# Loading the first and fourth conditioning blocks in two pieces each, with fewer constant products at the head

## The chip, the cores and the metric

The kernel runs on one NeuronCore of a Trainium2 chip. A core has five engines that run at the same time: TensorE (PE in the profile, with its weight loads as PEld), VectorE (DVE), ScalarE (ACT), GpSimd (POOL) and SyncE (SP). Sixteen DMA engines move data between HBM and the core's memory SBUF. A queue of loads is issued by SP, a few by ACT and POOL. The metric is device time in microseconds (us) of one execution; lower is better.

## The reference

One inference step of a one-layer decoder, for 256 prompt tokens and 8 x 4 sample tokens (T = 288 columns in the kernel), model width 2048, everything in float32:

```python
def _layer(x, c, conv_prefix, chunk, ...):
    mod = (jax.nn.silu(c) @ w_ada + b_ada).reshape(n, N_MOD, 1, D_MODEL)
    sh_m, sc_m, gt_m, sh_f, sc_f, gt_f = [mod[:, i] for i in range(N_MOD)]
    h = _rms(x, g_mix) * (1 + sc_m) + sh_m
    proj = h @ w_in                      # 2048 x 9216
    b_gate, c_gate, hc, u, v, ga, gb = jnp.split(proj, idx, axis=-1)
    z = c_gate * hc
    conv = sum(w_conv[k] * zfull[:, k:k + s] for k in range(CONV_WIDTH))
    ya = b_gate * conv
    ...                                  # yb: gated spatial mixing of u and v
    merged = jax.nn.sigmoid(ga) * (ya @ w_pa) + jax.nn.sigmoid(gb) * (yb @ w_pb)
    x = x + gt_m * (merged @ w_out)
    h2 = _rms(x, g_ffn) * (1 + sc_f) + sh_f
    gate, up = jnp.split(h2 @ w_ffn_in, 2, axis=-1)
    x = x + gt_f * ((jax.nn.silu(gate) * up) @ w_ffn_out)
    return x, conv_state, v_rows
```

There are nine conditioning vectors `c` (one for the prompt, eight for the samples). `silu(c) @ w_ada` is 9 x 2048 by 2048 x 12288; the rest of the layer needs its columns as scales, shifts and gates.

## The kernel before

Activations lie with features on the 128 partitions and tokens along the free dimension. Every large product is made in three passes: weight and activation are each cut into a high part (a copy rounded to fp32r) and a low part (the rest), and PE adds high x high, high x low and low x high in PSUM. ACT casts the high part (`hi`), DVE subtracts for the low part (`lo`).

The weights stream from HBM in blocks. Blocks of `w_in` are called wA, wB, wC, wE, wD (`Blk`), those of `w_ada` aA, aB, aC, aE, a2 to a5 (`Ada`). A block is loaded into one of five buffers named `raw` (RAW = 5). The list `steps` gives the order of the blocks and of the work between them (`Do`). A load is issued five blocks ahead of its use. Up to the step `free`, the instructions of DVE and ACT keep the order in which the code issues them, and those of SP do so still longer (`Pinned`); PE's order is chained as well (`S["pe"]`, `strict`). Behind these points the framework orders what is not chained.

The head is what the change touches:

- `ct`, the nine vectors (128 x 144), is loaded by ACT's queue. `silu` makes `cs` of it: a tanh on ACT (`ctt`), two instructions on DVE.
- The aA blocks hold the columns of `w_ada` that give the scale and the shift of the first 128 features. There are four, each 128 partitions x 1024 columns (512 KB), and each is used in eight float32 products of 32 x 128 (`Ada.run`, L423), sixteen records in the trace. They go to four groups of 32 columns of PE, and all add into one PSUM tile `ada`.
- `aA[3].out` copies `ada` to `ev` on ACT; `early_weights` makes `b1` from the constants `cp1` and, in `wA[0].first`, `hi` and `lo` of the first 256 columns of the first weight block on DVE; `aA[3].fin` multiplies `ev` by a selection matrix (L456) and makes `gm1` (`gm` in the trace) and `mod` on DVE; `early0` scales the first 128 features of `x` by `gm1` and cuts them into `hi` and `lo` (`s`). Then `wA[0]` (`FirstBlk.run`, L674) makes the first projection products.
- `warm(n)` makes n products of a 128 x 128 matrix of ones with itself (L310), whose result nobody reads. Each stands as two records in the trace. With a second argument it is placed behind that instruction.

SP issues the loads in this order: the four aA blocks, `cp1`, the first 512 columns of wA[0], the first part of `x`, the rest of wA[0], and then the blocks of `steps`.

The functions that the diff touches and what calls them:

Of the kernel before, what the change touches and what calls it, by code (L numbers as in the profile page):

```python
# [68 lines left out]
def decoder_kernel(tc, d):  # L69
    nc = tc.nc  # L70
    with ExitStack() as es:
        def pool(name, bufs=1, **kw):
            return es.enter_context(tc.tile_pool(name=name, bufs=bufs, **kw))

        pc = pool("const")
        pw = pool("wstream")
        pslot = pool("slots", SLOTS)
        ptmp = pool("tmp", 5)
        pps = pool("psum", 4, space=bass.MemoryType.PSUM)
        early = ExitStack()  # L80
        pshort = early.enter_context(tc.tile_pool(name="short", bufs=SHORT, side="right"))

        def reopen():
            early.close()
            return pool("thirds", 2, side="right", reuse_waits="tile")

        _body(tc, nc, d, pc, pw, pslot, pshort, reopen, ptmp, pps)


def _body(tc, nc, d, pc, pw, pslot, pshort, reopen, ptmp, pps):  # L90
    ids = [0]

    def nm(s):
        ids[0] += 1
        return f"{s}_{ids[0]}"
# [4 lines left out]
    def slot(dt=F32, shape=(P, T), short=False):  # L100
        return (pshort if short else pslot).tile(list(shape), dt, tag="s", name=nm("s"), padded_shape=[P, TU])
# [7 lines left out]
    def psmisc():  # L109
        return pps.tile([P, 512], F32, tag="misc", name=nm("px"), bufs=3)  # L110

    def behind(i):
        return tc.issue_after(i.ins) if i is not None else ExitStack()
# [17 lines left out]
    V, A, G, PE, SY = Pinned(nc.vector), Pinned(nc.scalar), nc.gpsimd, nc.tensor, Pinned(nc.sync)  # L131
# [174 lines left out]
    def warm(n, after=None):  # L306
        ps = psmisc()
        with behind(after):
            for _ in range(n):
                PE.matmul(ps[:, :P], ones, ones, start=True, stop=True)  # L310
# [75 lines left out]
    class Ada(Step):  # L386
# [7 lines left out]
        def load(self):  # L394
            self.ks = 2 if self.fb[0] == self.fb[1] else 1
            if self.apart:
                self.raw = [slot(shape=(P, 256)) for _ in range(8)]
                for i, t in enumerate(self.raw):
                    SY.dma_start(t, d[self.name][self.blk][:, 256 * i : 256 * i + 256])
                return  # L400
            n = self.nk * 512 * self.nq // self.ks
            self.raw = pw.tile([P, n], F32, tag="raw", name=nm("raw"), bufs=RAW, padded_shape=[P, 2048])
            SY.dma_start(self.raw, d[self.name][self.blk])

        def split(self):
            pass
# [307 lines left out]
    def ada(name):  # L714
        u = units[name]
        return [(Thirds if name == "a5" else Ada)(u, b) for b in range(16 // u[3])]
# [540 lines left out]
    aA, aB, aC, aE = (ada(n) for n in ("aA", "aB", "aC", "aE"))  # L1257
# [59 lines left out]
        for k in range(1, 4):  # L1317
            mo[k].norm()

    steps = [Do(silu), Do(lambda: warm(10)), *aA[:2], Do(lambda: warm(1, aA[1].last)), aA[2]]  # L1320
    steps += [Do(lambda: warm(2, aA[2].last)), aA[3], Do(lambda: warm(1, aA[3].last)), Do(aA[3].out), Do(early_weights), Do(aA[3].fin), Do(early0)]
    steps += [Do(lambda: warm(5, aA[3].last))] + wA[:4] + aB[:2] + [wA[4], Do(sums1), Do(sums1_out)] + aB[2:4] + [Do(rstd1), wA[5]]
    steps += aB[4:6] + [wA[6], Do(norms)] + aB[6:] + wA[7:] + [Do(free), *wB[:2]]
    steps += aC[:2] + [wB[2], Do(later), rescale(LONG, RAWX, "rbl"), rescale(0, 10, "rbl")] + aC[2:4] + wB[3:4] + [norms_ahead(4, 8)] + begin(wB[4]) + aC[4:6] + wB[4:5] + begin(wB[5]) + aC[6:] + [wB[5], gain(4, 8)]
# [89 lines left out]
    n = len(steps)  # L1414
# [174 lines left out]
```

## Time and profile before

| | |
|---|---|
| median of 3 runs | 1514.07 us (1513.61 to 1514.92) |
| profiled execution, its time | 1513.66 us |
| profiled execution, its span (first to last instruction) | 1511.9 us |
| granted TensorE clock | 0.999 |
| PE busy | 1504.7 us |
| DVE busy | 1060.9 us |
| ACT busy | 776.5 us |
| POOL busy | 176.6 us |
| HBM read | 352.56 MB |

The profile is of one execution. The span runs from the first to the last instruction; the time of an execution is 1.76 us more. Busy time of PE counts every matrix product, useful or not, and products are pipelined, so a busy PE says only that something was in it. In rows of the chain stand start, length, engine, tile, line of the code and the number of records; rows of the timeline add the shapes, and in brackets the idle time before the instruction and what ended it. Line 124 is a helper that most DVE, ACT and SP instructions pass through, so these are told apart by their tiles.

### The profile page before, as it was taken

How to read it: one execution, taken by the hardware profiler on the slowest of the kernel's cores; microseconds unless marked ns; L12 is line 12 of the kernel's file. 1: busy time of each engine (PE TensorE's matmuls, PEld its weight loads, DVE VectorE, ACT ScalarE, POOL GpSimd, SP SyncE). 2: the span in 40 equal slices, each digit the busy share in tenths (PEclk: the TensorE clock that was granted, in tenths of full speed). 3: DMA queues.
4: the chain of work that ended last, by engine and by line, in shares of the span. 5: the costliest groups of instructions: out<-in, count | busy, mean ns of one | idle time of the engine just before them, and what ended most of it. 6: DMA issues, size and time to landing. Idle time of an engine off the chain costs nothing.

```text
span 1511.9 us, 32334 instructions
## 1 busy us (share of the span) xinstructions
PE 1504.7 (100%) x12734; PEld 1449.6 (96%) x12734; DVE 1060.9 (70%) x2099; ACT 776.5 (51%) x1487; POOL 176.6 (12%) x353
## 2 busy tenths in 40 slices
PE   9999999999999999999999999999999999999998
PEld 8898999998899898989999999999999999999998
DVE  6786677978666576667878666666666567675586
ACT  5443354743345444457655455455545454454465
POOL 2555410000030000002500101100010100100000
PEclk9999999999999999999999999999999999999999
DMA  9977876578888778875654657564575745754452
GB/s 390 357 282 301 344 272 219 197 285 313 328 321 311 261 258 299 272 278 204 225 190 163 218 189 244 205 215 142 180 248 183 251 136 178 243 186 157 146 176 98
DMA packets 75689, 357.75 MB, mean 237 GB/s; under 512 B 9248, under 2 KB 28512, under 8 KB 46352
## 3 DMA queue, kind: packets, MB, share of 16 engines
q1 hardware_dynamic: 70384, 337.02, 62.4%
q0 software_dynamic: 5008, 18.59, 3.5%
q8 instruction: 99, 1.62, 0.4%
q14 instruction: 54, 0.44, 0.1%
q10 hardware_dynamic: 144, 0.07, 0.0%
HBM read 352.56 MB, written 3.09 MB: 235 GB/s over the span
## 4 chain that ended last, share of the span: by engine, by line
PE 100%; DVEq 0%; DVE 0%; issue 0%
PE pm L575 30%; PE pm L577 30%; PE pm L576 30%; PE ada L423 5%; PE ada L630 1%; PE px L304 1%; PE px L310 0%; PE pm L690 0%; PE pm L692 0%; PE pm L691 0%; PE pm L674 0%; PE px L733 0%; PE px L692 0%; PE px L691 0%; PE px L690 0%; PE pm L304 0%
## 5 line engine op out<-in xcount | busy, mean ns | idle before, releaser
L575 PE MATMUL pm<-s,hi 128*128 128x288 f32 (+1 forms) x3688 | 1058.1, 287 | 0.0
L577 PE MATMUL pm<-s,lo 128*128 128x288 f32 (+1 forms) x3688 | 1055.0, 286 | 0.0
L576 PE MATMUL pm<-s,hi 128*128 128x288 f32 (+1 forms) x3688 | 1054.9, 286 | 0.0
L124 ACT CAST hi<-raw 128x512 fp32r<-128x512 f32 (+2 forms) x956 | 578.4, 606 | 633.7 <-PE pm L576 547.1
L124 DVE TENSOR_TENSOR lo<-raw,hi 128x512 fp32r<-128x512 f32 (+2 forms) x959 | 657.2, 691 | 333.5 <-ACT hi L124 310.8
L575 PEld LDWEIGHTS pm<-s,hi 128*128 128x128 f32 x3688 | 697.0, 189 | 10.8 <-issue 8.9
L576 PEld LDWEIGHTS pm<-s,hi 128*128 128x128 f32 x3688 | 697.1, 189 | 0.0
L577 PEld LDWEIGHTS pm<-s,lo 128*128 128x128 f32 x3688 | 697.0, 189 | 0.0
L124 DVE TENSOR_TENSOR s<-pm,s 128x288 f32<-128x288 f32 x175 | 78.8, 454 | 24.8 <-PE pm L577 20.5
L594 POOL DMA_DIRECT2D s<-in_a x64 | 34.1, 538 | 344.7 <-PE pm L577 327.2
L423 PE MATMUL ada<-raw,cs 128*32 128x512 f32 (+3 forms) x640 | 61.8, 515 | 0.0
L124 ACT CAST s<-t 128x288 fp32r<-128x288 f32 (+2 forms) x109 | 50.3, 465 | 18.2 <-DVE t L124 15.4
L124 DVE TENSOR_TENSOR s<-t,s 128x288 fp32r<-128x288 f32 (+1 forms) x109 | 50.1, 462 | 10.7 <-ACT s L124 10.4
L124 DVE SCALAR_TENSOR_TENSOR t<-t,pm 128x288 f32<-128x288 f32 x84 | 37.9, 451 | 12.5 <-PE pm L577 8.5
L423 PEld LDWEIGHTS ada<-raw,cs 128*32 128x32 f32 x640 | 18.7, 112 | 25.3 <-issue 17.3
L124 DVE TENSOR_TENSOR s<-s,s 128x256 f32<-128x256 f32 (+2 forms) x96 | 38.4, 430 | 0.5 <-ACT s L124 0.5
L315 POOL TENSOR_TENSOR t<-x,gm 128x32 f32<-128x32 f32 x16 | 7.7, 483 | 262.5 <-DVE acc L124 248.4
L124 ACT CAST s<-s 128x256 bf16<-128x256 f32 (+1 forms) x80 | 29.7, 414 | 1.8 <-DVE s L124 1.8
L803 POOL TENSOR_TENSOR s<-s,rb 128x288 f32<-128x288 f32 x30 | 29.1, 991 | 0.0
L599 POOL DMA_DIRECT2D word<-in_a x8 | 4.4, 549 | 196.4 <-PE ada L630 142.8
L124 DVE SCALAR_TENSOR_TENSOR s<-pm,s 128x288 f32<-128x288 f32 x48 | 24.3, 511 | 2.5 <-PE pm L577 2.5
L124 ACT COPY s<-pm 128x288 f32<-128x288 f32 (+1 forms) x53 | 21.1, 401 | 9.1 <-PE pm L577 8.5
(189 smaller groups left out, 721.2 us busy)
## 6 DMA issues: line engine op xcount, KB each, us to landing
raw<-in_fi SPq DMA_DIRECT2D x84, 1024.0 KB, 4.9
raw<-in_f SPq DMA_DIRECT2D x64, 704.0 KB, 4.1
raw<-in_wD SPq DMA_DIRECT2D x36, 1024.0 KB, 8.3
raw<-in_a SPq DMA_DIRECT2D x32, 1024.0 KB, 5.1
raw<-in_wC SPq DMA_DIRECT2D x20, 896.0 KB, 6.1
raw<-in_aE SPq DMA_DIRECT2D x16, 1024.0 KB, 7.5
s<-in_a SPq DMA_DIRECT2D x128, 128.0 KB, 5.2
raw<-in_wo SPq DMA_DIRECT2D x16, 1024.0 KB, 6.7
```

The lines of the kernel that those rows point to most:

```text
L124: i = f(*args, **kw)
L304: return in_order(op(*args, **kw))
L315: G.tensor_tensor(sam(a[:, TP:T]), sam(x[:, k, TP:]), bc4(gm[:, k, 1:]), ALU.mult)
L423: PE.matmul(acc[32 * j : 32 * j + 32, c], cs9[:, 32 * kt : 32 * kt + 32] if second else cs[:, kt, :], self.raw[2 * j + h] if self.apart el ...
L575: PE.matmul(ps[:, : self.n], wh, ah, start=first, stop=False)
L576: PE.matmul(ps[:, : self.n], wh, al, start=False, stop=False)
L577: self.last = in_order(PE.matmul(ps[:, : self.n], wl, ah, start=False, stop=last))
L594: G.dma_start(w, src[:, 256 * i : 256 * i + 256])
L599: G.dma_start(raw, src)
L630: PE.matmul(acc[32 * j : 32 * j + 32, n * h : n * h + n], S["csr"][:, self.blk, :], w[:, o : o + n], start=self.blk == 0 and p == 0, stop= ...
L803: G.tensor_tensor(a[:, :T], a[:, :T], S[rb], ALU.mult)
```

## The change

The load of an `Ada` block that is not cut into slots is issued in pieces where a table says so: aA[0] as columns 0 to 256 and 256 to 1024, aA[3] as columns 0 to 512 and 512 to 1024. All other blocks are loaded in one piece as before. The number of constant products at the very start goes from ten to eight, and before aA[3] from two to one.

```diff
@@ Ada.load
             n = self.nk * 512 * self.nq // self.ks
             self.raw = pw.tile([P, n], F32, tag="raw", name=nm("raw"), bufs=RAW, padded_shape=[P, 2048])
-            SY.dma_start(self.raw, d[self.name][self.blk])
+            cuts = {("aA", 0): [0, 256, n], ("aA", 3): [0, 512, n]}.get((self.name, self.blk), [0, n])
+            for a, b in zip(cuts, cuts[1:]):
+                SY.dma_start(self.raw[:, a:b], d[self.name][self.blk][:, a:b])
@@ steps
-    steps = [Do(silu), Do(lambda: warm(10)), *aA[:2], Do(lambda: warm(1, aA[1].last)), aA[2]]
-    steps += [Do(lambda: warm(2, aA[2].last)), aA[3], Do(lambda: warm(1, aA[3].last)), Do(aA[3].out), ...
+    steps = [Do(silu), Do(lambda: warm(8)), *aA[:2], Do(lambda: warm(1, aA[1].last)), aA[2]]
+    steps += [Do(lambda: warm(1, aA[2].last)), aA[3], Do(lambda: warm(1, aA[3].last)), Do(aA[3].out), ...
```

More of the change, by code (lines that the diff above doesn't have):

```diff
@@ L1318, in norms @@
             mo[k].norm()
-    steps = [Do(silu), Do(lambda: warm(10)), *aA[:2], Do(lambda: warm(1, aA[1].last)), aA[2]]
-    steps += [Do(lambda: warm(2, aA[2].last)), aA[3], Do(lambda: warm(1, aA[3].last)), Do(aA[3].out), Do(early_weights), Do(aA[3].fin), Do(early0)]
+    steps = [Do(silu), Do(lambda: warm(8)), *aA[:2], Do(lambda: warm(1, aA[1].last)), aA[2]]
+    steps += [Do(lambda: warm(1, aA[2].last)), aA[3], Do(lambda: warm(1, aA[3].last)), Do(aA[3].out), Do(early_weights), Do(aA[3].fin), Do(early0)]
     steps += [Do(lambda: warm(5, aA[3].last))] + wA[:4] + aB[:2] + [wA[4], Do(sums1), Do(sums1_out)] + aB[2:4] + [Do(rstd1), wA[5]]
```

## The prediction

> **What bounds the kernel now.** I read the page's busy table and its chain first, then the chain, the timeline and the DMA issues of the first 12 us, where the change lies.
>
> ```profile
> PE 1504.7 (100%) x12734; PEld 1449.6 (96%) x12734; DVE 1060.9 (70%) x2099; ACT 776.5 (51%) x1487; POOL 176.6 (12%) x353
> PE 100%; DVEq 0%; DVE 0%; issue 0%
> ```
>
> TensorE (PE) is busy for 1504.7 of 1511.9 us and the chain that ends last is PE throughout. So the change can move the end only by as much as it moves the start of the dense work, and only if nothing later takes that back. The head, as the chain tells it (start, length, what):
>
> ```profile
> 1.05 4.63 PE px L310 x20
> 5.69 1.61 PE ada L423 x32
> 7.30 0.42 PE px L310 x2
> 7.72 0.57 PE ada L423 x16
> 8.29 0.64 PE px L310 x4
> 8.93 0.57 PE ada L423 x16
> 9.51 0.42 PE px L310 x2
> 9.93 0.36 PE px L456 x2
> 10.29 1.21 PE px L310 x10
> 11.50 3.18 PE pm L674 x24
> ```
>
> L310 is the constant product (two records each), L423 the conditioning blocks aA (the first row holds aA[0] and aA[1]), L456 the product that puts their result into columns, L674 the first projection block, where the dense work begins. A busy PE here is partly filler, so the chain hides what really sets 11.5. Behind the filler the other engines show it (start, length, engine, instruction, idle before and its releaser):
>
> ```profile
> 4.67 0.32 ACT L124 ACTIVATE ctt<-ct 128x144 f32<-128x144 f32 x1 [2.22 <-DMA ct<-in_c]
> 5.37 0.23 DVE L124 TENSOR_SCALAR cs<-ctt 128x144 f32<-128x144 f32 x1
> 9.22 0.29 DVE L124 CAST hi<-raw 128x256 fp32r<-128x256 f32 x1 [0.53 <-DMA raw<-in_wA]
> 9.55 0.43 DVE L124 TENSOR_TENSOR lo<-raw,hi 128x256 fp32r<-128x256 f32 x1
> 9.57 0.27 ACT L124 COPY ev<-ada 128x128 f32<-128x128 f32 x1 [4.58 <-PE ada L423]
> 10.33 0.23 DVE L124 SCALAR_TENSOR_TENSOR gm<-px,b,cp 128x9 f32<-128x9 f32 x1 [0.35 <-PE px L456]
> 10.59 0.53 ACT L124 ACTIVATE s<-x,gm 128x256 fp32r<-128x256 f32 x1 [0.45 <-DVE gm L124]
> 11.08 0.23 ACT L124 CAST s<-t 128x42 fp32r<-128x42 f32 x1
> 11.36 0.39 PE L674 MATMUL pm<-s,hi 128*128 128x298 f32 x1
> ```
>
> Two chains meet in `gm` at 10.33. One goes from the landing of `ct` over the tanh and `cs` (ready at 5.60) to the four aA blocks, `ev` and L456. The other is VectorE's (DVE's) own order: the first weight block lands, `hi` and `lo` are made (9.22 to 9.98), then `gm`. The first chain is late by 0.35 us today. From `gm` to the first L674 product pass 1.03 us of fixed work.
>
> The loads (issue on SP; then each load with the time from issue to landing):
>
> ```profile
> 0.74 1.80 SPq L124 DMA_DIRECT2D raw<-in_aA  x4
> 2.58 0.54 SPq L124 DMA_DIRECT2D cp<-in_cpack  x1
> 3.17 0.49 SPq L124 DMA_DIRECT2D raw<-in_wA  x1
> 3.70 0.44 SPq L124 DMA_DIRECT2D x<-in_x  x1
> ct<-in_c ACTq DMA_DIRECT2D x1, 72.0 KB, 3.9
> raw<-in_aA SPq DMA_DIRECT2D x1, 512.0 KB, 3.7
> raw<-in_aA SPq DMA_DIRECT2D x1, 512.0 KB, 6.2
> raw<-in_wA SPq DMA_DIRECT2D x1, 256.0 KB, 6.0
> x<-in_x SPq DMA_DIRECT2D x1, 144.0 KB, 5.9
> SPq L124 <- DMA ct<-in_c: 0.5, 1, 0.5
> ```
>
> The 3.7 is aA[0]'s, landed at 4.44; the 6.2 is aA[3]'s, issued last of the four at 2.11 and landed at 8.3; `wA` landed at 3.17 + 6.0 = 9.2, `x` at 9.6. The tanh starts at 4.67, so `ct` landed at about 4.65, only 0.2 after aA[0] though it has a seventh of its bytes. The next view has busy time by engine, then the granted clock, the DMA share and GB/s:
>
> ```profile
> 1.50:2.50 1.00, 1.00 (x7) 1.00 (x7) 0.06 (x1) 0.95 (x1) 0.00 (x0) 1.00 0.69 136
> 2.50:3.50 1.00, 1.00 (x6) 1.00 (x6) 0.00 (x0) 0.00 (x0) 0.00 (x0) 1.00 0.88 315
> 3.50:4.20 0.70, 0.70 (x5) 0.70 (x4) 0.00 (x0) 0.00 (x0) 0.00 (x0) 1.00 1.08 421
> 4.20:9.20 5.00, 5.00 (x73) 4.02 (x76) 0.70 (x3) 0.32 (x1) 0.00 (x0) 1.00 1.02 403
> ```
>
> The DMA engines are full from 3.5 us on: whatever stands in line lands when the bytes ahead of it have passed.
>
> **The change part by part.** *aA[0] in 256 and 768 columns.* `ct` (72 KB) travels beside a first piece of 128 KB instead of 512 KB. The latest it can land is as now, 4.65. The earliest: the windows moved 0.14 MB by 2.5 us, 0.45 by 3.5 and 0.75 by 4.2, so aA[0] and `ct` together (0.60 MB) were through at about 3.85, and `ct` was landed 0.8 later; 0.2 MB would be through at 2.7, landed at 3.5. Its landing beside aA[0]'s says that the two advanced together, row by row, so it should follow the shorter rows, but part of it will meet the 768-column rows. I take the middle, 4.05. From `ct` to aA's first product pass 5.69 - 4.65 = 1.04 us, so that starts at 5.1 (bounds 4.55 and 5.7). The second piece lands with the same bytes as now, about 4.5, in time.
>
> [...]
>
> *Ten constant products become eight.* The first row of the chain gives 4.63 / 20 = 0.23 us a record, so the filler ends 4 x 0.23 = 0.9 earlier, at 4.76. Today it ends at 5.68, `cs` is ready at 5.60: they are level. Eight products leave PE idle from 4.76 to 5.1, and to 5.7 if `ct` does not move. This alone frees nothing.
>
> *Two constant products before aA[3] become one.* 0.64 - 0.42 = 0.22 us out of the aA chain, if aA[3]'s data is there.
>
> *aA[3] in halves.* It lands at 8.3 now, and its products start at 8.93. With the chain 0.6 earlier they would wait; with halves the first 256 KB (0.65 us earlier at 403 GB/s) lets half of them run, and only the second half waits for 8.4.
>
> *Two more loads on SP.* 1.80 / 4 = 0.45 us each, so `cp1`, `wA` and `x` are issued 0.9 later (wA at 4.07). The line of bytes ahead of them covers this: `wA` waits 6 us in line. Uncovered it would cost that 0.9. SP also stood 0.5 us for `ct` before the ninth load (the last row of the loads); with two more that wait meets `wA`'s first piece, at 4.05 against an issue at 4.07: nothing, and 0.6 in the worst case, still 3 us ahead of its turn. What is not covered is the loss from shorter rows. Below, it is nothing or a gain (the bytes are the same, and the start might fill sooner). Above: if the start is paid by rows, the first 128 rows carry 128 KB where they carried 512, and 0.39 MB at 403 GB/s is 0.96 us on every landing behind. I take 0.1, since from 2.5 us on the rate rose to 315 and 421 with `ct`'s short rows in the mix.
>
> *The sum.* aA[0] and aA[1] run at half pace, 0.85 each (a little over half of the 1.61 that their 32 records took, since the pace stepped up at their end): 5.1 to 6.8. Then one product 0.42, aA[2] 0.57, one product 0.42: 8.2. aA[3] ends at the later of 8.2 + 0.57 and its second half's landing 8.4 + 0.4 (half of its work and its tail): 8.8, against 9.5 now. L456 ended at 10.29, 0.8 behind aA[3], so it ends 0.7 earlier, at 9.6. But `gm` stands behind `hi` and `lo`: `wA` at 9.2 + 0.1, then 0.76 of DVE work: 10.08. So `gm` moves by 10.33 - 10.08 = 0.25 us and not by 0.7, and the first L674 product starts at 11.11. The five products behind L456 are then finished well ahead.
>
> Behind that every order stays as it is, and PE is the chain. Loads that could take it back lie between 12 and 52 us, where the DMA engines are full. The tightest I found is the second aB block (issue, its landing after 12.1 us, and the products):
>
> ```profile
> 11.78 0.33 SPq L124 DMA_DIRECT2D raw<-in_aB  x1
> raw<-in_aB SPq DMA_DIRECT2D x1, 768.0 KB, 12.1
> 23.76 1.50 PE L423 MATMUL ada<-raw,cs 128*32 128x384 f32 x16
> ```
>
> It lands at 23.9; its half of the 16 records starts near 24.4. With PE 0.25 earlier and the load 0.1 later, 0.15 or more is left. So the gain is 0.25 us: the profiled execution, 1513.66 (1.76 more than its span), becomes 1513.4; it lies 0.4 below the median of the runs, 1514.07. My time is 1513.8.
>
> **The rivals.** *The deeper gain.* If `wA` lands sooner (a quicker start), `gm` follows L456: 0.7 less, 1513.4. For it: the first chain really is 0.7 shorter. Against: `wA` stands behind 2.1 MB in a full line. Chance 0.1.
>
> *Nothing arrives.* `ct` lands as now, aA starts at 5.7, and of the first chain only the 0.22 is left; L456 ends at 10.07 and `gm` runs at 10.1. Oddly that is the forecast's time too, since DVE decides; if short rows cost 0.35 us instead of 0.1, it is 1514.1, no change. Chance 0.22.
>
> *Slower by the start of the loads.* The upper bound above, 0.96 us on `wA`: `hi` at 10.2, `gm` at 10.95, 0.6 later than now: 1514.7. It decides from a delay of 0.35 us on. For it speaks the slow first microsecond (136 GB/s), against it that `ct`'s 576-byte rows passed in that same stretch. Chance 0.15.
>
> *Slower by PE's pace.* The granted clock in the rows reads 1.00 throughout, yet ten records of the constant product took 1.21 us after 10.3 and 2.3 (20 in 4.63) before 5.7: PE runs at half pace until some point during aA[1]. The idle stretch that eight products leave may put that point off. At half pace from 5.1 to the end of aA: 6.8 for two blocks, about 0.65 for each product with its switch, 0.85 for aA[2] and aA[3]: 9.8, `gm` at 10.6, 0.3 later than now; if it reaches into L674's 24 products (3.18 us), up to 3.2 more. So 1514.4 to 1517.6. Chance 0.13. [...]
>
> **How the numbers follow.** Forecast 0.40, the others as given: 1.0. The lowest run shown, 1513.61, less 0.9 for the deeper gain gives 1512.7; the highest, 1514.92, with 0.5 of the slower cases gives 1515.4. A measurement of this kernel tells about 0.2% from no change, 3.0 us, and no case but the far end of the slow pace leaves that: 0.03 slower, 0.02 faster (only by an order that shifts far behind the head, which I can't see), 0.95 within.
>
> **What would show it.** In the changed profile: the tanh at about 4.1 instead of 4.67; aA's first product near 5.1 with PE idle before it for some 0.3 us; the 32 records still at half pace; `ev` near 8.9; `hi` waiting for `wA` at 9.3, `gm` with no wait for L456 at 10.1; the first L674 product near 11.1 and PE idle before it. I am wrong if the tanh stays at 4.67, if `hi` starts after 9.6, if the records of aA[2] are still at half pace, or if PE waits for a load between 12 and 52 us.

## The result and the profile after

The changed kernel takes 1516.69 us (median of 22 runs, 1514.30 to 1520.07), the kernel before 1514.44 us beside it (22 runs, 1513.61 to 1517.46): a ratio of 1.0015 [1.0008, 1.0022]. It is slower by about 2.2 us, 0.15%, which is within the 0.2% that the prediction called no change, but its time, 1513.8 us, and its range up to 1515.4 lie below what was measured. Not only the median moved: the executions of the changed kernel spread over 5.8 us.

The profiled execution of the changed kernel took 1516.54 us, its span is 1514.7 us. The busy row of PE and the chain by engine, from its page:

```profile
PE 1505.0 (99%) x12728; PEld 1448.9 (96%) x12728; DVE 1060.9 (70%) x2099; ACT 775.5 (51%) x1487; POOL 177.9 (12%) x353
...
PE 98%; DMA 1%; SPq 0%; ACT 0%; DVE 0%; issue 0%; DVEq 0%; ACTq 0%
```

PE's busy time is what it was (1504.7 before), while the span is 2.8 us longer: PE got no more work, it waited, and on the chain stands DMA with 1% where before there was none. (Line numbers have moved by two: L425 is the line of the conditioning products that was L423, L458 was L456, L676 was L674, L447 was L445.)

The head, first from the timeline (start, length, engine, instruction, idle before it and what ended that), then from the chain (start, length, what):

```profile
3.21 0.32 ACT L124 ACTIVATE ctt<-ct 128x144 f32<-128x144 f32 x1 [0.76 <-DMA ct<-in_c]
...
4.77 1.08 PE L425 MATMUL ada<-raw,cs 128*32 128x128 f32 x16
...
6.08 1.04 PE L425 MATMUL ada<-raw,cs 128*32 128x128 f32 x16 [0.22 <-DMA raw<-in_aA]
...
8.45 0.68 PE L425 MATMUL ada<-raw,cs 128*32 128x128 f32 x16
9.20 0.27 ACT L124 COPY ev<-ada 128x128 f32<-128x128 f32 x1 [5.66 <-PE ada L425]
...
9.62 0.29 DVE L124 CAST hi<-raw 128x256 fp32r<-128x256 f32 x1 [0.52 <-DMA raw<-in_wA]
...
10.30 0.22 DVE L124 SCALAR_TENSOR_TENSOR gm<-px,b,cp 128x9 f32<-128x9 f32 x1
```

```profile
4.22 5.38 DMA raw<-in_wA
...
11.32 3.31 PE pm L676 x24
```

`ct` came 1.46 us earlier (tanh at 3.21 instead of 4.67), the first conditioning product 0.9 earlier. But the second block made PE wait for 0.22 us, and the weight block wA landed at 9.60 (4.22 + 5.38) instead of 9.20. With that `gm` starts at 10.30 instead of 10.33 and the first projection product at 11.32 instead of 11.36. Of the whole change the head kept 0.04 us.

The line of loads shows why. Windows (length, busy time of PE, PEld, DVE, ACT, POOL, then the granted clock, the DMA share and GB/s), the first two rows from the kernel before, the other three from the changed one:

```profile
3.50:4.25 0.75, 0.75 (x6) 0.75 (x5) 0.00 (x0) 0.00 (x0) 0.00 (x0) 1.00 1.07 420
4.25:5.50 1.25, 1.25 (x7) 1.14 (x6) 0.44 (x2) 0.32 (x1) 0.00 (x0) 1.00 1.02 416
```

```profile
3.50:4.25 0.75, 0.75 (x6) 0.75 (x5) 0.55 (x2) 0.04 (x1) 0.00 (x0) 1.00 1.06 317
4.25:5.50 1.25, 1.25 (x19) 0.89 (x18) 0.00 (x0) 0.00 (x0) 0.00 (x0) 1.00 0.99 387
5.50:8.00 2.50, 2.28 (x42) 1.27 (x34) 0.00 (x0) 0.00 (x0) 0.00 (x0) 1.00 1.02 379
```

The engines are as full as before (DMA share about 1), yet they move a quarter less where the second block begins: its packets take longer (those of 4 KB up to 0.55 us in that stretch, and 0.16 in the kernel before). By the rows of the prediction the kernel before is slow up to 3.5 us only; the changed one is still slow behind that.

The 2.8 us of this execution's span do not stand in the head, though. The longest wait is at 195 us (chain of the changed kernel, then ACT's timeline there, then the same rows and the product of L445 before):

```profile
188.53 6.78 DMA raw<-in_wC
...
195.93 0.59 ACT ev L124
...
196.56 0.66 PE px L447 x4
```

```profile
195.41 0.62 ACT L124 CAST hi<-raw 128x512 fp32r<-128x512 f32 x1 [7.44 <-DMA raw<-in_wC]
195.93 0.58 ACT L124 COPY ev<-ada 128x512 f32<-128x512 f32 x1
```

```profile
192.72 0.62 ACT L124 CAST hi<-raw 128x512 fp32r<-128x512 f32 x1 [5.15 <-DMA raw<-in_wC]
193.46 0.59 ACT L124 COPY ev<-ada 128x512 f32<-128x512 f32 x1
...
194.32 0.44 PE px L445 x4
```

A wC block took 6.78 us from issue to landing. Its cast stands ahead of `ev` in ACT's order, so `ev` waited with it, and PE waited for `ev`. Before, the cast ended at 192.72 + 0.62 = 193.34, just 0.12 us ahead of `ev`. This place had hardly any slack, and the load arrived 2.7 us later in this execution (195.41 against 192.72). PE came to the product behind `ev` 2.2 us late (196.56 against 194.32).

So there were three things to tell apart: late loads at the head, late loads farther on, and PE's clock, since the mean granted clock of 8 of the 22 executions was 0.998 or less (one of 141 of the kernel before in the comparisons that follow).

### The profile page after: what moved, and what is told of

Read it like the earlier page. It is cut to its first block, busy times and chain, and to the rows that moved or that the text cites. A ratio compares the mean times of both kernels' runs of the same rounds, so it can differ in the third digit from the quotient of the medians.

```text
span 1514.7 us, 32324 instructions
## 1 busy us (share of the span) xinstructions
PE 1505.0 (99%) x12728; PEld 1448.9 (96%) x12728; DVE 1060.9 (70%) x2099; ACT 775.5 (51%) x1487; POOL 177.9 (12%) x353
## 3 DMA queue, kind: packets, MB, share of 16 engines
q8 instruction: 99, 1.62, 0.4%
## 4 chain that ended last, share of the span: by engine, by line
PE 98%; DMA 1%; SPq 0%; ACT 0%; DVE 0%; issue 0%; DVEq 0%; ACTq 0%
PE pm L577 30%; PE pm L579 30%; PE pm L578 30%; PE ada L425 4%; PE ada L632 1%; PE px L304 1%; DMA raw<-in_wC 0%; PE pm L692 0%; PE pm L694 0%; PE pm L693 0%; DMA raw<-in_wA 0%; PE pm L676 0%; SPq L124 0%; PE px L735 0%; PE px L694 0%; PE px L692 0%
## 5 line engine op out<-in xcount | busy, mean ns | idle before, releaser
L425 PE MATMUL ada<-raw,cs 128*32 128x512 f32 (+3 forms) x640 | 62.5, 517 | 0.2 <-DMA raw<-in_aA 0.2
L425 PEld LDWEIGHTS ada<-raw,cs 128*32 128x32 f32 x640 | 19.0, 112 | 25.7 <-issue 17.9
```

Source lines behind the costliest of these rows:

```text
L425: PE.matmul(acc[32 * j : 32 * j + 32, c], cs9[:, 32 * kt : 32 * kt + 32] if second else cs[:, kt, :], self.raw[2 * j + h] if self.apart el ...
```

## The experiments

Each was measured beside the kernel before, whose median was 1514.34 us beside e1 to e4, 1514.67 beside e5 to e8, 1514.44 beside e9 to e12, 1514.78 beside e13 and e14, and 1514.46 beside e15 and e16. The ratios are those on record; they differ somewhat from the quotients of the medians (e5: 1.0014, and 1.0008 by the medians). My theory at the start was that a cut of the first block disturbs the start of the loads; the rivals were that the products taken away move PE against the loads of its own code, that one late load near 195 us makes the loss, and that the clock does.

**Which part does it.** Four kernels have one part each:

```diff
# e1_split_only: the two cuts; products as before (10; 1, 2, 1)
# e2_products_only: 8 products and 1; the loads as before
# e5_first_only: before, and
+ cuts = {("aA", 0): [0, 256, n]}.get((self.name, self.blk), [0, n])
# e6_fourth_only: before, and
+ cuts = {("aA", 3): [0, 512, n]}.get((self.name, self.blk), [0, n])
```

> The two loads in pieces as in the change, the constant products as before (10, 1, 2, 1, 5). Theory A (PE's code): the page lists 99 packets of 16 KB on the instruction queue, about one for each 257 records of PE and PEld; three constant products fewer are 12 instructions fewer, so each later piece of code is fetched at another moment against the loads. Here PE's instructions are those of before, so A expects the time of before: 1514.4 (1513.8 to 1515), the profile without a wait of PE near 195 us. Theory B (the pieces themselves: shorter rows, two more loads in the line, wA landing 0.4 later) expects the time of after: 1516.7, with the wait.

> The products of the change (8 and 1), all loads whole as before. A expects the slow time: 1516 to 1517 with a spread of some us, and a load of wC or aE that lands 1.5 us or more behind what its bytes need. B expects 1514.2 to 1514.5, as before.

> Only the first block in pieces (256 and 768 columns), the fourth whole, products as before. The profiles so far show a second slow stretch of the loads when aA[1] begins, 3.5 to 4.25 us, in every kernel with the pieces (191 to 317 GB/s, against 420 in before), and in three of four of them one DMA engine then 1.2 to 2 us behind, so that aA[1] and all loads behind it land late. Theory C (the cut of the first block brings that second slow stretch): about 1516.5, as with both cuts, and aA[1] landing after 7 us. Theory D (each further load in the line costs its part): about 1515.4, half of it.

> Only the fourth block in halves, the first whole, products as before. C expects the time of before, 1514.2 to 1514.6, with 400 GB/s or more in 3.5 to 4.25 us; D expects about 1515.4.

| | median, us | ratio to before |
|---|---|---|
| e1: both cuts | 1516.50 | 1.0015 [1.0006, 1.0024] |
| e2: products only | 1514.77 | 1.0005 [0.9996, 1.0014] |
| e5: first block cut | 1515.89 | 1.0014 [1.0005, 1.0023] |
| e6: fourth block cut | 1515.11 | 1.0006 [0.9997, 1.0015] |

The first block's cut alone is clearly slower, 1.2 us by the medians, and with the fourth's it gives the whole loss, 2.2 us. The products alone and the fourth cut alone are 0.4 us above before, with intervals that include no change. e1 has PE's products as before, so the theory of PE's code falls. Its head (windows, PE's wait, the chain):

```profile
3.50:4.25 0.75, 0.75 (x6) 0.75 (x5) 0.54 (x2) 0.11 (x1) 0.00 (x0) 1.00 0.92 223
4.25:5.50 1.25, 1.25 (x7) 1.14 (x6) 0.00 (x0) 0.00 (x0) 0.00 (x0) 1.00 0.90 341
```

```profile
PE ada L425 <- DMA raw<-in_aA: 1.4, 2, 1.2
```

```profile
12.80 3.32 PE pm L676 x24
```

223 GB/s where the kernel before has 420: the stretch is slower than in the change's own profile, PE waits 1.4 us for the blocks, and the first projection product starts at 12.80 instead of 11.36. e5's is alike: 262 GB/s in the first of the two windows, the first projection product at 12.22. In e1 a single DMA engine makes most of the wait: fifteen of the sixteen parts of the second block had landed by 6.39, the last landed at 7.64.

e2's profile shows another way in which the head can come late (PE's third block, then `gm`):

```profile
8.50 1.08 PE L423 MATMUL ada<-raw,cs 128*32 128x128 f32 x16
11.50 0.23 DVE L124 SCALAR_TENSOR_TENSOR gm<-px,b,cp 128x9 f32<-128x9 f32 x1 [0.53 <-PE px L456]
```

With eight products, and `ct` landing as late as before, PE was idle for 1.06 us ahead of the first conditioning block. The products of the third block still took 1.08 us there, and 0.64 in the kernel before: PE's half pace of the start lasted until past 9.5 us, where it had ended by 7.3. `gm` waited for L456, and the first projection product started at 12.53. The granted clock reads 1.00 from 5.5 to 8 us all the same, so this start does not show in the mean clock of its execution.

**PE's number of instructions, and the late load at 195 us.** e3 puts three small products behind the eight, so that PE has its old number of instructions. e4 puts the copy `ev` ahead of the cast that waits for wC; e7 does that in the kernel before.

```diff
# e3_refill: the change, and
-     steps = [Do(silu), Do(lambda: warm(8)), ...
+     steps = [Do(silu), Do(lambda: warm(8, None, 3)), ...     # 3 of 16 columns
# e4_ev_first: the change, and (e7_before_ev_first: the kernel before, and); Ada.out also keeps its copy as self.copied
+     wC[17].defer = True
+     def split17():
+         with behind(aE[-1].copied):
+             wC[17].split()
-     for v in weave(paced, [[u] for u in visits(aE, 4, gain(8, 16))], 2, 15)[:-4]:
+     for v in weave(paced, [[u] for u in visits(aE, 4, Do(split17), gain(8, 16))], 2, 15)[:-4]:
```

> The change, and behind its eight constant products three small ones with 16 columns, which bring PE's number of instructions back to that of before and lie in the idle stretch before aA. A expects 1514.2 to 1514.8, spread as before; B expects 1516.7, since the pieces are there.

> The change, and on ACT the copy of the last aE result goes ahead of the first cast of the wC block whose load landed late (in the profile of after ACT waited 7.4 us for that load with the copy behind it, and PE 1.84 us for the copy). If that wait is the main place where the time goes, the median falls from 1516.7 to about 1515 and the highest runs with it. If late loads hit at several places, only part of it comes back: 1516, with the spread kept.

> The kernel before, with the copy of the last aE result ahead of the first cast of the next wC block on ACT. With the change under this order the runs at full clock fell together at 1514.6 to 1515.1. If late loads behind that cast also make the upper part of before's spread, the median falls by 0.1 to 0.3 to about 1514.1 and runs over 1515.5 become rare; if not, 1514.4 with the spread of before.

e3: 1518.22 us, 1.0021 [1.0012, 1.0030], not cured. e4: 1516.33, 1.0015 [1.0006, 1.0024], e7: 1514.58, 1.0003 [0.9994, 1.0012]: the order at 195 us gives neither kernel anything that can be told from nothing. So the wait that was longest in the changed kernel's profile is not the whole loss. Whether it is a part of it stays open.

But e4's profile caught the worst head (PE's wait, then windows):

```profile
PE ada L425 <- DMA raw<-in_aA: 2.7, 1, 2.7
```

```profile
4.00:6.00 2.00, 1.46 (x20) 0.80 (x19) 0.26 (x2) 0.00 (x0) 0.00 (x0) 1.00 0.88 331
6.00:8.00 2.00, 0.00 (x0) 0.00 (x0) 0.00 (x0) 0.00 (x0) 0.00 (x0) 0.85 0.98 376
8.00:10.00 2.00, 1.81 (x22) 1.17 (x26) 0.00 (x0) 0.00 (x0) 0.00 (x0) 0.50 1.07 395
...
14.00:16.00 2.00, 2.00 (x11) 2.00 (x11) 1.90 (x9) 1.23 (x3) 0.00 (x0) 0.50 0.98 377
16.00:18.00 2.00, 2.00 (x12) 2.00 (x10) 0.67 (x2) 0.41 (x2) 0.64 (x2) 0.59 1.02 407
```

```profile
13.74 2.31 PE px L310 x10
16.06 3.88 PE pm L676 x24
```

PE waits 2.7 us for the second block, fifteen of whose sixteen parts had landed by 6.16, the last at 8.14; in that wait the granted clock falls to half and stays there past 16 us. The five products that took 1.21 us before take 2.31, and the first projection product starts 4.6 us late (16.06 in the chain, against 11.50). e3's profile shows the same with a wait of 2.2 us. e4's executions fall in two groups: four with a clock of 0.999 or more at 1514.63 to 1515.08, seven with 0.998 or less at 1515.96 to 1519.31. By an estimate from e4's windows that is the size to be expected: at half clock for 10 us, 5 of some 1515 us are lost in the mean, 0.003. In e1's profile waits of 1.4 us together, the longest 1.2, left the clock at 1.00. Of the change's own 22 executions with a clock of 0.999 or more, e11's included, 12 lie above the highest of e4's four; four are too few to say whether the order at 195 us takes such times away.

**Is the clock the loss?** e9 gives PE four more products while it waits for the second block; e11 is the change once more, beside it.

```diff
# e9_keep_busy: the change, and
-     steps = [Do(silu), Do(lambda: warm(8)), *aA[:2], ...
+     steps = [Do(silu), Do(lambda: warm(8)), aA[0], Do(lambda: warm(4, aA[0].last)), aA[1], ...
```

> The change, and four more constant products between the first and the second conditioning block, so that TensorE has work while the second block is awaited. If half of the change's cost is TensorE's clock falling back after it has waited over 2 us for a late load, the wait shrinks by the four products' 0.9 us or more, the long times of 1518 to 1520 go, no execution shows a mean clock of 0.998 or less, and the median is 1515.5 to 1516: the late loads themselves still cost about 1 us. If the clock has nothing to do with it, the spread up to 1519 to 1520 stays and the median is 1516.7, or higher by the products' own time.

> The change once more, unaltered, beside the other kernels on one chip. By the late loads at the start: 1516.3 to 1517.0, with times up to 1519 or 1520, and in the profile TensorE waits 0.2 to 2.5 us for the second or the third conditioning block, the first weight block landing between 9.6 and 11.5. By the theory that the loss is the late load near 190 us alone: the same time, but the head as in the first profile of the change (weight block landed at 9.6) and TensorE idle for some 2 us near 195.

e9: 1516.29 us (1514.57 to 1518.01), 1.0011 [1.0002, 1.0020]. The low clock is rarer (1 execution of 11, against 11 of 33 in the two measurements of the change, which chance alone would give in about one case of eight), and no time is above 1518.1, as 9 of those 33 are; the median does not improve on e11: 1515.88 us (1514.17 to 1518.50), 1.0012 [1.0003, 1.0021]. So the clock is a part of the loss and not all of it. Of the change's 33 executions the 11 with a clock of 0.998 or less have a median of 1517.84, the other 22 one of 1515.52, which is still 1 us above the kernel before; and four of the nine times above 1518.1, the longest (1520.07) among them, have a clock of 0.999 or 1.000. What made those four long no profile shows; a start like e2's would not stand in this clock. My 1515.5 to 1516 for e9 was missed. e11 came out lower than the change's first 1516.69, as far as 11 such spread runs can tell. Its profile shows the late loads (246 GB/s from 3.5 to 4.25 us; the chain's row):

```profile
4.68 5.82 DMA raw<-in_wA
```

The weight block landed at 10.50, 1.3 later than before, the first projection product started at 12.22.

**Which property of the cut does it.** e8 cuts the first block in halves of 512 columns, e10 by partitions into two pieces of whole 4 KB rows; e12 is the change without the first cut; e13 cuts the second block instead of the first; e14 cuts nothing, but loads `ct` on SP's queue behind the first block instead of on ACT's beside it.

```diff
# e8_first_halves: before, and
+ cuts = {("aA", 0): [0, 512, n]}.get((self.name, self.blk), [0, n])
# e10_by_rows: before, and for aA[0] pieces [0:64] and [64:128] of the partitions
+ SY.dma_start(self.raw[a:b], d[self.name][self.blk][a:b])
# e12_no_first_cut: the change, and
+ cuts = {("aA", 3): [0, 512, n]}.get((self.name, self.blk), [0, n])
# e13_second_cut: before, and
+ cuts = [0, 256, n] if (self.name, self.blk) == ("aA", 1) else [0, n]
# e14_ct_in_line: before, and
-     A.dma_start(ct, d["c"])
      for s in aA:
          s.load()
+         if s is aA[0]:
+             SY.dma_start(ct, d["c"])
```

> The first block in two halves of 512 columns, the fourth whole, products as before. If short rows are what makes the second slow stretch, this lies between before and the cut at 256: 1514.4 to 1516, with 300 to 400 GB/s in 3.5 to 4.25 us. If any cut of the first block does it, 1516.5.

> The kernel before, with its first conditioning block loaded in two pieces too, but cut by partitions: 64 whole rows of 4 KB, then the other 64; products as before. If short rows at the start are what makes the second slow stretch of the loads, this one has none: 1514.4 to 1514.8, 400 GB/s or more from 3.5 to 4.25 us, the second conditioning block landed by 6.0. If any additional load at that place does it, 1515.5 or more and 250 to 350 GB/s in that stretch. Fewer rows in flight for each of the two loads could cost 0.2 by itself.

> The change without the cut of the first block: eight products and one, the fourth block in halves. If the first block's short rows carry the cost, 1514.4 to 1515.0 and no execution with a mean clock of 0.998 or less. If the parts add (0.4 for the products, 0.45 for the fourth block's halves, as each measured by itself), 1515.2. If the short rows are not the cause, 1516 to 1517 as with the whole change.

> The kernel before with one cut moved: the first conditioning block whole, the second in 256 and 768 columns. As many loads, rows and bytes as with the first block cut, and the third block issued at the same time; only the place differs. If an additional load or shorter rows anywhere at the head cost the microsecond, 1515.5 to 1516 and a stretch below 350 GB/s after 3.5 us. If the cost belongs to the start, where a load is reached soon after it was issued and its first packets are slow, this cut is harmless: 1514.4 to 1514.8, some 400 GB/s from 3.5 us on, the first weight block landed by 9.6.

> The kernel before, all blocks whole, with the conditioning vectors ct loaded on SP's queue behind the first conditioning block instead of on ACT's queue beside it. If the packets of ct that run beside the second block are what covers the slow start of that block in the kernel before, the stretch from 3.5 us on falls to 250 to 350 GB/s here too though no block is cut, the weight block lands at 10 or later, and the median is 1515.5 or more. If only the cut itself does it, 400 GB/s from 3.5 us on, and the time is 1514.4 to 1514.9, with SP's issues behind ct 0.45 later.

| | median, us | ratio to before |
|---|---|---|
| e8: first block in column halves | 1515.53 | 1.0007 [0.9999, 1.0016] |
| e10: first block by partitions | 1515.88 | 1.0010 [1.0001, 1.0019] |
| e12: the change without the first cut | 1515.19 | 1.0005 [0.9996, 1.0014] |
| e13: second block cut | 1515.74 | 1.0006 [0.9997, 1.0015] |
| e14: `ct` in line, nothing cut | 1516.90 | 1.0012 [1.0002, 1.0021] |

Their windows from 3.50 to 4.25 and 4.25 to 5.50, of e8, e10, e13 and e14 in this order:

```profile
3.50:4.25 0.75, 0.75 (x6) 0.75 (x5) 0.00 (x0) 0.32 (x1) 0.00 (x0) 1.00 1.10 440
4.25:5.50 1.25, 1.25 (x11) 1.13 (x14) 0.55 (x2) 0.00 (x0) 0.00 (x0) 1.00 0.94 338
```

```profile
3.50:4.25 0.75, 0.75 (x6) 0.75 (x5) 0.10 (x1) 0.00 (x0) 0.00 (x0) 1.00 1.05 284
4.25:5.50 1.25, 0.86 (x7) 0.67 (x6) 0.00 (x0) 0.00 (x0) 0.00 (x0) 1.00 0.93 256
```

```profile
3.50:4.25 0.75, 0.75 (x6) 0.75 (x5) 0.00 (x0) 0.00 (x0) 0.00 (x0) 1.00 1.01 375
4.25:5.50 1.25, 1.25 (x7) 1.15 (x6) 0.22 (x1) 0.32 (x1) 0.00 (x0) 1.00 1.17 392
```

```profile
3.50:4.25 0.75, 0.75 (x6) 0.75 (x5) 0.00 (x0) 0.00 (x0) 0.00 (x0) 1.00 0.95 344
4.25:5.50 1.25, 1.25 (x7) 1.15 (x6) 0.54 (x2) 0.32 (x1) 0.00 (x0) 1.00 0.95 367
```

e8 has the full rate where the second block begins, and that block landed at 5.61 (5.73 in the kernel before); the rate falls behind it, and the third block landed at 8.11 instead of 6.98. So the slow stretch does not always stand at the second block. e10 has no short row and is slow in both windows: short rows are not needed for it, against what I expected. e13 has as many loads and short rows as a first cut and nearly the old rates, and its weight block landed at 9.67: at the head the place seems to count, as far as one profile tells. Its median lies 1 us above before all the same, with an interval that includes no change; its profile has PE waiting elsewhere (1.1 us for a conditioning block near 171 us), so its total says little of the head. e14 disturbs the start without any cut: two of the sixteen parts of the third block came late (at 8.18 and 8.25, the fourteenth at 7.43), the weight block landed at 10.34, and 3 of 11 executions have a clock of 0.998 or less.

**Packets beside the second block.** In the kernel before, `ct`'s packets run beside the first blocks until 4.17 us; in the change they are through at 2.92, before the second block begins, and in line (e14) they are issued ahead of it. e15 therefore loads `cp1` on ACT's queue behind `ct`, in the change; e16 does so in the kernel before.

```diff
      A.dma_start(ct, d["c"])
+     A.dma_start(cp1, d["cpack1"])
      for s in aA:
          s.load()
-     SY.dma_start(cp1, d["cpack1"])
```

> The change, with the constants cp1 (128 rows of 664 bytes) loaded on ACT's queue behind ct instead of on SP's queue behind the aA blocks, so that short packets of a second queue run beside the second block again, after ct is through. If such packets are what keeps the start of that block fast, 380 GB/s or more from 3.5 us on, the second block landed by 6.2, no execution with a mean clock of 0.998 or less, and 1514.4 to 1515.0. If the cut does the harm whatever runs beside it, the stretch stays at 250 to 330 GB/s and the median at 1515.9 to 1516.7. Between the two, if cp1 covers a part only.

> The kernel before, with cp1 on ACT's queue behind ct. The same bytes stand ahead of the first weight block, and one issue fewer. If a longer second stream steadies the start, the kernel before loses its slower executions of 1515.5 and more: 1513.8 to 1514.3. If a whole first block needs no such cover, as before: 1514.4 to 1514.8. A second transfer on ACT's queue could also push the tanh back by 0.1 to 0.3, which the constant products ahead of the first block don't cover: 1514.9.

e15: 1515.54 us, 1.0009 [1.0000, 1.0018], 3 of 11 executions at a low clock; e16 has 408 GB/s from 3.5 to 4.25 us, but it gains nothing: 1514.29, 1.0000 [0.9991, 1.0009]. e15's windows:

```profile
3.50:4.25 0.75, 0.75 (x6) 0.75 (x5) 0.54 (x2) 0.09 (x1) 0.00 (x0) 1.00 0.95 348
4.25:5.50 1.25, 1.16 (x7) 0.48 (x6) 0.00 (x0) 0.00 (x0) 0.00 (x0) 1.00 0.94 325
```

A second queue's packets did not bring the old rate (420 and 416 GB/s) back. That explanation falls as well. No version beats the kernel before.

**All starts side by side.** One profile is little, since the starts vary: e7 is the kernel before up to 190 us, and its weight block landed at 9.88 instead of 9.20; in e2, whose loads are whole, one of the sixteen parts of the third block came 0.84 us behind the other fifteen (8.06 and 7.22). Taken together, the profiles still differ. In the seven with a whole first block and `ct` on ACT's queue (before, e2, e6, e7, e12, e13, e16) the weight block landed at 9.2 to 10.2 us, 9.8 in the median; in the ten with a cut first block (the change, e1, e3, e4, e5, e8, e9, e10, e11, e15) at 9.6 to 11.6, 10.5 in the median. In e14 it was 10.3.

What stays open: why the loads come late behind a cut first block. Short rows are not needed for it (e10), an additional load at the second block does not bring it (e13), and company for the queue does not take it away (e15). But one rival was not tested: all ten kernels with a cut first block, and e14, issue one more load ahead of the second block, which so goes out at about 1.65 us (2.0 in e10) instead of 1.2; e13 does not. No run tells this delay from the cut itself. And a part of the loss stands behind the head, at waits near 170, 195 and 344 us that differ from execution to execution. From the first projection product to the end of the span pass 1500.5 us in the kernel before, 1501.0 in e1, 1501.9 in e5 and e11 and 1503.4 in the change's own profile, but also 1501.7 in e16, whose median is that of the kernel before; one profile for each kernel can't say how much of it the change brings about.

## Why the prediction was wrong

*What bounds the kernel.* Right: PE, busy for 1505.0 of 1514.7 us. Beside the head and the waits for loads, PE's clock moved the end too (1517.84 us in the median of the change's executions with a clock of 0.998 or less, 1515.52 in that of the others).

*`ct` comes earlier.* Right in kind; it landed at about 3.2, before the 3.5 to 4.65 that I had bounded. The first conditioning product started at 4.77 instead of 5.1, PE idle from 4.63. Shorter rows beside it are not needed for that: in e10, whose first block comes in whole 4 KB rows, `ct` landed 1.9 us after its issue, in the change 2.5, in the kernel before 3.9.

*`gm` is held by the weight block and not by the conditioning chain.* Right: `ev` was ready at 9.47, `gm` ran at 10.30 behind `hi` and `lo`, with no wait for the product of L458.

*The loss from shorter rows.* This is the step that failed. "I take 0.1, since from 2.5 us on the rate rose to 315 and 421 with `ct`'s short rows in the mix": the rows of the kernel before told of a start with a whole first block, and I carried their rate over to one that is cut. The weight block landed 0.4 later in the change's own profile, 1.3 in its second (and in e5's), 1.9 in e1's, 2.4 in e4's. Even my upper bound, 0.96, was too small, since it priced bytes that travel in the first slow microsecond, and the loss comes behind it: packets take longer there, whole 4 KB rows included (up to 0.55 us, against 0.16), and single parts of a load fall back (in e1 the last part of the second block landed at 7.64, the other fifteen by 6.39). The landing that I added to, 9.20, was also the earliest of all the profiles with a whole first block (9.8 in the median), so 0.4 alone would not tell the change from chance; 10.5, the median with a cut first block, does. And the sum counted on late loads for the weight block and, with 0.1, the fourth conditioning block, while the head's chain runs through a late second or third block in e1, e4 and e5. With 0.4 in place of 0.1 the sum gives 10.36 for `gm`, about what the profile shows, and no gain; `hi` started at 9.62, past the 9.6 that I had named as a sign of being wrong. With 1.3 the sum gives a loss of 0.9, which is that of the heads of e5 and e11 (12.22 against 11.36).

*The cover farther on.* "Loads that could take it back lie between 12 and 52 us" was too narrow. The place without slack in the changed kernel's profile was at 195 us: 0.12 us in the kernel before, far behind the stretch that I had priced.

*The rivals.* "Slower by the start of the loads" had the mechanism, at 0.15; its 1514.7 was too low for the reason above. "Slower by PE's pace" had the clock, at 0.13, and its 1514.4 to 1517.6 holds the measured time. Its trigger, the idle stretch that eight products leave, was a guess that no row of the kernel before shows. In the change's own profile that stretch is 0.14 us and did nothing; in e2 it is 1.06 us, and the half pace lasted past 9.5 us (in e12, with 1.62 us, it did not last longer: 50 records in 1.92 us of busy PE from 5.5 to 8 us, against 33 in 2.09 in e2; so the stretch alone does not decide it). The trigger that I had not seen is the wait for a late block: within waits of 2.2 us (e3) and 2.7 us (e4) the clock fell to 0.50. There the two rivals are one chain, and I priced each of them without the other.

*Faster, same, slower.* The 0.95 for within 0.2% was right (1.0015); the direction was not.

## What to carry to other kernels

The first loads of this kernel were a special case: how the queue started with one whole block (420 GB/s from 3.5 to 4.25 us) did not say how it starts with a cut one (317 and 246 in the change's two profiles), so bound a cut there from both sides by a whole landing time, not by the bytes, and take that time from several profiles: here it varied by 1 us without any cut of the first block (9.2 to 10.2). When PE has little to do but wait at the head, price a late load twice, once for its wait and once for the clock that may fall in it (e4: 2.7 us, then a clock of 0.50), and keep filler where that wait stands, which may hold the clock though not the landing (e9: one low clock in 11 executions, against 11 in 33, and the weight block at 9.95). And don't take the longest new wait of one profile for the whole cause: a second profile of the same kernel (e11 waited 0.2 us there instead of 1.8) costs less than the wrong story.

## What the runs showed of the hardware

In e3 and e4 PE waited 2.2 and 2.7 us for the second block; in that wait the granted clock fell to 0.50, and it stayed there for about 7 and 10 us although PE was nearly always busy (e4: from 7.4 to 17.6 us, with PE busy for 1.81 to 2.00 of every 2 us from 8 us on). And a full line did not keep its rate: with the engines' share at 0.9 and more, they moved 223 (e1) to 440 GB/s (e8) from 3.5 to 4.25 us. PE waited for the last of a load's sixteen parts: e14's third block had fourteen at 7.43 and the last at 8.25, and its products began at 8.29; e4's second block had fifteen by 6.16 and the last at 8.14, and its products began at 8.19.
